# The first chunk's up projection, from seven products of halves to full blocks

## The chip, the cores and the metric

The kernel runs on one core of one Trainium2 chip. The metric is the device time of one execution in microseconds (us), lower is better. The kernel before was timed three times: 1994.26 us median, 1993.06 to 1998.03. A separate profiled execution gives the traces that are read here. Five engines take part: PE (TensorE, the matrix multiplier, whose weight loads are listed apart as PEld), DVE (VectorE), ACT (ScalarE), POOL (GpSimd, idle here) and SP, whose queue issues every DMA of this kernel.

## The reference

One layer of a hybrid decoder over 16 meta tokens and 2048 tokens of width 1024, in float32:

```
h = concat(meta, x)
u = rmsnorm(h, mix_norm_g);  p = u @ w_in                    # W: 1024 -> 1792
y = concat(pool_mixer(p), conformer_conv(p), rglru_branch(p))  # the mixers
h = h + y @ w_out                                            # O
u = rmsnorm(h, mlp_norm_g)                                   # norm2
h = h + square(relu(u @ w_up)) @ w_down                      # U: 1024 -> 4096, D: 4096 -> 1024
out = rmsnorm(h, final_norm_g)[:, 16:]
```

## The kernel before

Everything is held transposed, channels on the 128 partitions and tokens along the free axis. The tokens go in four chunks of 512 (the first also carries the 16 meta tokens). Each chunk passes through W (14 blocks of 128 output channels), the mixers, O (8 blocks), norm2, then four groups g0 to g3, each of U (8 blocks) and D (8 blocks that add onto `h`). The order of these items is written out in the list `items`: W of chunks 0 and 1, O 0, the last three W blocks of chunk 1, then U and D of chunk 0, O 1, W 2, U and D of chunk 1, O 2, and so on. U1 below is U of chunk 1, O1 is O of chunk 1.

Precision is kept by splitting each float32 operand into a rounded high part and a rest (`split`: ACT copies to `hi`, DVE subtracts to get `lo`). A block product is then three matmuls for each of 8 steps of depth: 24 matmuls of 128x512 (`mm_tile`, L278; the first two blocks of a D group go through `mm_pair`, L292, which leaves the last two depth steps to the end). Weights arrive by SP as 128x512 tiles `wr` (6 buffers) and are split into `wh` (4 buffers) by ACT (L110) and DVE (L111). A block needs two such tiles.

U is done otherwise. `up_unit` computes two blocks of 128 channels at once by Strassen's scheme in Winograd's form: seven products of quarter size instead of eight, 12 matmuls of 128x256 each (`mm_block`, L302). It needs sums of the up weights, which `gen_sums` builds on DVE during chunk 0 (L196, L197, L201, L202), stores to DRAM as `sums` and which SP then loads again as weights: of a unit's seven weight tiles four are `sums`. It also needs 14 operand tiles, made by `gen_norm2` (L731 normalises, L738 forms sums, L111 splits), and after the products DVE additions in PSUM order (L795, L820) before ReLU, two squares and one subtraction (L801 to L804) give the two tiles `U` that D reads. Each unit holds four PSUM tiles in use one after the other, and its later products wait for the additions of DVE.

The mixers and the sums are written as generators that hand out pieces of DVE and ACT work. After each item `pump(budget)` draws pieces until their nominal ns use the budget up: 5000 for a W or O item, 3000 for a D item, 150 for a U unit. The list `urgent` comes first (norm2, the sums, the split of the mixers' outputs `gen_ysplit`, the final norm, the next chunk's inputs `gen_x`), the mixers `Mix` after it. At the last U of a chunk `need_mix` issues whatever is left of the next chunk's mixers. Sums for units 0 to 3 are put on the list at O 0, for the next four after each group of U of chunk 0. A scheduler then moves instructions on each engine, so the order below is read from the built program.

At O, `evac_o` adds each block to a tile `xr` of the residual (two buffers, shared with `gen_x`, which loads the chunk after next); `gen_final` stores the finished chunk through the same SP queue.

Of the kernel before, what the change touches and what calls it, by code (L numbers as in the profile page):

```python
# [31 lines left out]
D = 1024  # L32
KB = D // P
# [46 lines left out]
def build(nc, tc, x0, xr, w_in, w_out, w_fold, w_up, w_down, vecs, gates, pools, pws, out):  # L80
# [109 lines left out]
    def gen_sums(u):  # L190

        a11, a12, a21, a22 = (t_(t, W0, n)[:, :512] for t, n in (("s", SBF), ("t", TB), ("t", TB), ("s", SBF)))
        for t, m, c0 in ((a21, 1, 0), (a22, 1, 512), (a11, 0, 0), (a12, 0, 512)):
            nc.sync.dma_start(out=t, in_=w_up[2 * u + m][:, c0 : c0 + 512])
        yield 0
        V.tensor_tensor(out=a22, in0=a21, in1=a22, op=ALU.add)  # L196
        V.tensor_tensor(out=a21, in0=a11, in1=a21, op=ALU.subtract)  # L197
        nc.sync.dma_start(out=sums[u][:, 1536:2048], in_=a22)
        nc.sync.dma_start(out=sums[u][:, 1024:1536], in_=a21)
        yield 1400  # L200
        V.tensor_tensor(out=a11, in0=a22, in1=a11, op=ALU.subtract)  # L201
        V.tensor_tensor(out=a12, in0=a12, in1=a11, op=ALU.subtract)  # L202
        nc.sync.dma_start(out=sums[u][:, 0:512], in_=a11)
        nc.sync.dma_start(out=sums[u][:, 512:1024], in_=a12)
        yield 1400
# [512 lines left out]
    def gen_norm2(o):  # L718
# [54 lines left out]
        for p in range(2):  # L773
            put("B22", p, b22[p])
            put("T4", p, b21[p])
            yield 1400

    def up_unit(o, u, h0):

        fa, fb = a_tile(), a_tile()  # L780
        o.f += [fa, fb]
        ra, rb, t2 = (t_("fr", W0, FR)[:, :NT] for _ in range(3))
        p1 = t_("q", 256, 2)
        order = ("B11", "B21", "T2", "T1", "T3", "B22", "T4")
        nxt = [h0]

        def product(ps):
            h = nxt[0]
            nxt[0] += 1
            wts.ahead(h)  # L790
            mm_block(ps, wts.hl.pop(h), o.u2[order[h - h0]])

        def add2(out, ps, x):

            V.tensor_tensor(  # L795
                out=out.rearrange("p (a c) -> p a c", a=2), in0=ps.rearrange("p (a c) -> p a c", a=2),
                in1=x.unsqueeze(1).broadcast_to([P, 2, 256]), op=ALU.add,
            )

        def square(f, r):  # L800
            A.activation(out=r, in_=r, func=AF.Relu)  # L801
            A.activation(out=f[:, 0], in_=r, func=AF.Square)  # L802
            A.activation(out=r, in_=r, func=AF.Square)  # L803
            V.tensor_tensor(out=f[:, 1], in0=r, in1=f[:, 0].bitcast(F32), op=ALU.subtract)  # L804

        px, py, pz = ps_main(), ps_main(), pw.tile([P, 1024], F32, name=nm("pw"), tag="pw")
        product(px[:, :256])
        A.activation(out=p1, in_=px[:, :256], func=AF.Copy)
        product(py[:, :256])
        product(py[:, 256:])  # L810

        add2(ra, py, p1)
        q = ra[:, 256:]
        product(pz[:, 512:768])
        product(pz[:, 768:])

        add2(t2, pz[:, 512:], q)
        px = ps_main()
        product(px[:, :256])
        V.tensor_tensor(out=q, in0=px[:, :256], in1=t2[:, :256], op=ALU.add)  # L820
        square(fa, ra)
        product(pz[:, 256:512])
        add2(rb, pz[:, 256:768], t2[:, 256:])
        square(fb, rb)

    def evac_d(o, g, j, ps, s0, s1):
# [39 lines left out]
    def pump(budget):  # L866
        credit[0] = min(credit[0], 0) + budget
        while credit[0] > 0:
            v = step()
            if v is None:  # L870
                break
            credit[0] -= v
# [24 lines left out]
    items.extend(("W", 1, b, full) for b in (3, 0, 1))  # L897
    for c in range(NCH):
        for g in range(FG):
            items.extend(("U", c, g * 4 + j, full) for j in range(4))  # L900
            down = [("D", c, g * KB + j, full) for j in range(KB)]
            if g < FG - 1 or c < 2:
                items.extend(down)
            elif c == 2:
                items.extend(down[:2])
                items.extend(("O", 3, j, full) for j in range(KB))
                items.extend(down[2:])
            else:
                for half in ((0, 256), (256, 512)):
                    items.extend(("D", c, g * KB + j, half) for j in range(KB))  # L910
        if c < 2:
            items.extend(("O", c + 1, j, full) for j in range(KB))
            items.extend(("W", c + 2, b, full) for b in range(14))

    def sources(it):

        kind, c, j, _ = it
        if kind == "U":
            m1, m2, s = w_up[2 * j], w_up[2 * j + 1], sums[j]
            aps = (  # L920
                (m1, 0), (m1, 512), (s, 0), (s, 1536), (s, 1024), (s, 512), (m2, 512),
            )
            return ("U", j), [lambda a=a, c0=c0: a[:, c0 : c0 + 512] for a, c0 in aps]
        if kind == "W":
            a = w_in[_WORDER[j][2]]
        elif kind == "D":
            a = w_down[j // KB, j % KB]
        else:
            return ("O", j), [lambda: wo_fold[j], lambda: w_out[j]]
        return (kind, a.offset if hasattr(a, "offset") else j, j), [lambda a=a, c0=c0: a[:, c0 : c0 + 512] for c0 in (0, 512)]  # L930

    srcs, windex, last = [], [], None
    for it in items:
        key, aps = sources(it)
        if it[0] == "W":
            key = ("W", _WORDER[it[2]][2])
        if key != last:
            first = len(srcs)
            srcs.extend(aps)
            last = key  # L940
        windex.append(first)
# [1 line left out]

    gx = {c: (gen_x if c else gen_x0)(ch[c]) for c in range(NCH)}
    gy = {c: gen_ysplit(ch[c]) for c in range(NCH)}
    gn = {c: gen_norm2(ch[c]) for c in range(NCH)}

    next(gx[0])
    mixes.append(Mix(ch[0]))
# [1 line left out]
    for n, it in enumerate(items):  # L951
        kind, c, j, (s0, s1) = it
        o = ch[c]
        if kind == "W":
            need(gx[c])
        elif kind == "O" and j == 0:
            if c == 0:
                urgent.append(gy[0])
            need(gy[c])
            need_mix()  # L960
        elif kind == "U":
            need(gn[c])
        wi = windex[n]
        if kind == "D" and j % KB == 1 and held_ps:
            evac_d(o, j // KB, j % KB, held_ps.pop(), s0, s1)
            pump(BUD_D)
            continue
        if kind == "D" and j % KB == 0 and s0 == 0:
            wts.ahead(wi)
            ws = [[wts.hl.pop(wi + 2 * i + q) for q in range(2)] for i in range(2)]  # L970
            pss = mm_pair(ws, o.f, (s0, s1))
            evac_d(o, j // KB, 0, pss[0], s0, s1)
            held_ps.append(pss[1])
            pump(BUD_D)
            continue
        if kind != "U":
            wts.ahead(wi)
            w = [wts.hl[wi], wts.hl[wi + 1]]
            if n + 1 == len(items) or windex[n + 1] != wi:
                del wts.hl[wi], wts.hl[wi + 1]  # L980
        if kind == "W":
            wk, i, _ = _WORDER[j]
            if n == 0:
                pss = mm_tile(w, o.x, subs_of(o, wk != "z"))
                for _ in gx[0]:
                    pass
                evac_w(o, wk, i, pss)
                urgent.append(gx[1])
                urgent.append(load_consts())
                urgent.append(gen_fold())  # L990
                continue
            evac_w(o, wk, i, mm_tile(w, o.x, subs_of(o, wk != "z")))
        elif kind == "O":
            evac_o(o, j, mm_tile(w, o.u, [full])[0])
            if j == 0 and c == 0:
                urgent.extend(gen_sums(u) for u in range(4))
            if j == KB - 1:
                urgent.append(gn[c])
        elif kind == "U":
            if j % 4 == 0:  # L1000
                o.f = []
            up_unit(o, j, wi)
            if j == 0 and c + 1 < NCH:
                mixes.append(Mix(ch[c + 1]))
            if c == 0 and j % 4 == 3 and j < NU - 1:
                urgent.extend(gen_sums(u) for u in range(j + 1, j + 5))
            if j == NU - 1 and c + 1 < NCH:
                need_mix()
                urgent.append(gy[c + 1])
        else:  # L1010
            ps = mm_tile(w, o.f, [(s0, s1)])[0]
            evac_d(o, j // KB, j % KB, ps, s0, s1)
            if j == FG * KB - 1:
                urgent.append(gen_final(o, s0, s1))
                if c + 2 < NCH:
                    urgent.append(gx[c + 2])
        pump({"U": BUD_U, "D": BUD_D}.get(kind, BUD0))
    while step() is not None:
        pass
    es.close()  # L1020
# [71 lines left out]
```

## Time and profile before

| | us |
|---|---|
| median of 3 runs | 1994.26 |
| profiled execution, its own time | 1989.49 |
| its span, first to last instruction | 1987.7 |
| PE busy in the span | 1927.7 |
| DVE busy | 1580.9 |
| ACT busy | 1127.3 |
| DMA moved | 297.77 MB |

Views of the trace give start and duration in us, the engine, the line of the kernel, the operation, the tile written and the tiles read, shapes and the count of merged instructions. A bracket at the end tells how long the engine stood idle before and what released it. Matmuls overlap, so a group's busy time over its count is longer than the spacing of two matmuls; spacing is read from the starts of following groups. A few per cent of the matmul records can be missing.

### The profile page before, as it was taken

The page shows a single profiled execution, that of the slowest core. Times are in us where ns is not written, and L with a number is a line of the kernel's source. Part 1 is how long each engine was busy: PE and PEld are TensorE (multiplying, and loading weights), DVE is VectorE, ACT ScalarE, POOL GpSimd, SP SyncE. Part 2 cuts the span into 40 slices and gives each one's busy share as a digit, 9 for nine tenths or more (in the row PEclk, how much of TensorE's full clock was granted, in tenths as well). Part 3 has the DMA queues.
Part 4 walks back from the last instruction along what each step waited for, and adds up shares of the span by engine and source line. Part 5 has one row for each costly group of instructions (what it writes and reads, how often), then busy time and mean ns, then how long its engine had stood idle before and what let it go on. Part 6 is the DMA issues. An engine that isn't in the chain of part 4 may idle for free.

```text
span 1987.7 us, 31314 instructions
## 1 busy us (share of the span) xinstructions
PE 1927.7 (97%) x11220; PEld 1685.3 (85%) x11220; DVE 1580.9 (80%) x2557; ACT 1127.3 (57%) x1907; POOL 0.2 (0%) x4
## 2 busy tenths in 40 slices
PE   8999999999999899999999999999999999999997
PEld 7888787888887689898988878988989889889897
DVE  7988787998979899984777689987668587656477
ACT  6575463636586445683666453675648446355364
POOL 0000000000000000000000000000000000000000
PEclk9999999999999999999999999999999999999999
DMA  6415578748443534353534543534445435545354
GB/s 196 133 53 189 181 254 267 254 124 270 125 130 90 186 100 147 110 161 94 165 113 142 172 135 93 163 106 149 132 127 151 135 102 158 162 143 149 112 175 144
DMA packets 166956, 297.77 MB, mean 150 GB/s; under 512 B 18320, under 2 KB 24592, under 8 KB 166800
## 3 DMA queue, kind: packets, MB, share of 16 engines
q1 hardware_dynamic: 166800, 295.77, 48.6%
q8 instruction: 88, 1.44, 0.3%
q14 instruction: 68, 0.56, 0.1%
HBM read 268.43 MB, written 27.26 MB: 149 GB/s over the span
## 4 chain that ended last, share of the span: by engine, by line
PE 73%; DVE 13%; DMA 5%; issue 4%; ACT 4%; SPq 0%; DVEq 0%; ACTq 0%
PE pm L278 41%; PE pm L302 13%; PE pw L302 11%; PE pm L292 7%; DVE wh L111 3%; DMA xr<-d_xr 2%; DMA s<-d_w_up 1%; DVE ca L534 1%; DVE fr L795 1%; ACT wh L110 1%; DVE t L568 1%; PE pb L311 1%; DVE H L111 0%; DVE h L828 0%; DVE U L804 0%
## 5 line engine op out<-in xcount | busy, mean ns | idle before, releaser
L110 ACT ACTIVATE wh<-wr 128x512 fp32r<-128x512 f32 x876 | 546.0, 627 | 669.7 <-PE pm L278 411.5
L278 PE MATMUL pm<-U,wh 128*128 128x512 f32 (+1 forms) x3504 | 790.2, 384 | 1.4 <-DVE wh L111 1.3
L278 PEld LDWEIGHTS pm<-U,wh 128*128 128x128 f32 x3504 | 634.7, 188 | 143.3 <-DVE wh L111 3.1
L111 DVE TENSOR_TENSOR wh<-wr,wh 128x512 fp32r<-128x512 f32 x876 | 598.5, 687 | 187.2 <-ACT wh L110 181.2
L302 PE MATMUL pm<-H,wh 128*128 128x256 f32 x3072 | 392.7, 283 | 4.7 <-DVE wh L111 2.9
L302 PEld LDWEIGHTS pm<-H,wh 128*128 128x128 f32 x3072 | 378.4, 189 | 9.2 <-DVE wh L111 4.4
L302 PE MATMUL pw<-H,wh 128*128 128x256 f32 x2304 | 301.4, 284 | 16.5 <-DVE fr L795 9.2
L302 PEld LDWEIGHTS pw<-H,wh 128*128 128x128 f32 x2304 | 284.9, 190 | 22.3 <-issue 7.2
L278 PE MATMUL pm<-H,wh 128*128 128x512 f32 (+1 forms) x1344 | 272.9, 361 | 13.5 <-ACT H L390 7.3
L278 PEld LDWEIGHTS pm<-H,wh 128*128 128x128 f32 x1344 | 227.7, 193 | 55.7 <-ACT H L390 7.3
L292 PE MATMUL pm<-U,wh 128*128 128x512 f32 (+1 forms) x768 | 176.5, 388 | 0.0
L292 PEld LDWEIGHTS pm<-U,wh 128*128 128x128 f32 x768 | 140.0, 188 | 30.9
L534 DVE SCALAR_TENSOR_TENSOR ca<-Pbv,vec,ca 128x512 f32<-128x512 f32 x180 | 127.0, 745 | 0.0
L828 DVE TENSOR_TENSOR h<-h,pm 128x512 f32<-128x512 f32 (+1 forms) x106 | 71.2, 674 | 49.7 <-PE pm L278 35.9
L804 DVE TENSOR_TENSOR U<-fr,U 128x512 fp32r<-128x512 f32 x128 | 87.3, 685 | 7.9 <-ACT fr L803 7.8
L801 ACT ACTIVATE fr<-fr 128x512 f32<-128x512 f32 x128 | 79.2, 621 | 25.2 <-DVE fr L820 22.5
L795 DVE TENSOR_TENSOR fr<-pw,fr 128x512 f32<-128x512 f32 x128 | 87.8, 686 | 5.5 <-PE pw L302 3.1
L802 ACT ACTIVATE U<-fr 128x512 fp32r<-128x512 f32 x128 | 79.3, 623 | 1.5
L803 ACT ACTIVATE fr<-fr 128x512 f32<-128x512 f32 x128 | 78.7, 618 | 0.3
L346 DVE TENSOR_TENSOR ss<-ss,fr 128x512 f32<-128x512 f32 (+1 forms) x84 | 54.0, 643 | 19.3 <-ACT fr L345 18.2
L337 DVE RECIPROCAL rs<-rs 128x512 f32<-128x512 f32 (+2 forms) x17 | 53.9, 3168 | 10.6 <-ACT rs L335 10.5
L795 DVE TENSOR_TENSOR fr<-pm,q 128x512 f32<-128x512 f32 x64 | 43.7, 683 | 2.8 <-PE pm L302 2.4
(202 smaller groups left out, 1136.3 us busy)
## 6 DMA issues: line engine op xcount, KB each, us to landing
wr<-d_w_down SPq DMA_DIRECT2D x272, 256.0 KB, 3.0
wr<-sums SPq DMA_DIRECT2D x256, 256.0 KB, 3.3
wr<-d_w_up SPq DMA_DIRECT2D x192, 256.0 KB, 3.0
wr<-d_w_in SPq DMA_DIRECT2D x92, 256.0 KB, 2.9
xr<-d_xr SPq DMA_DIRECT2D x56, 256.0 KB, 3.0
t<-d_w_up SPq DMA_DIRECT2D x32, 256.0 KB, 4.0
wr<-wo_fold SPq DMA_DIRECT2D x32, 256.0 KB, 2.7
wr<-d_w_out SPq DMA_DIRECT2D x32, 256.0 KB, 2.7
```

Source lines behind the costliest of these rows:

```text
L110: A.activation(out=hi, in_=src, func=AF.Copy)
L111: V.tensor_tensor(out=lo, in0=src, in1=hi.bitcast(F32), op=ALU.subtract)
L278: T.matmul(ps[:, : s1 - s0], w[k // 4][:, a, (k % 4) * P : (k % 4 + 1) * P], rhs[k][:, b, s0:s1], start=(k == 0 and j == 0), stop=(k == KB ...
L292: T.matmul(ps[:, : s1 - s0], w[k // 4][:, a, (k % 4) * P : (k % 4 + 1) * P], rhs[k][:, b, s0:s1], start=(k == 0 and j == 0), stop=(k == KB ...
L302: T.matmul(ps, w[:, a, k * P : (k + 1) * P], op[k // 2][:, b, (k % 2) * 256 : (k % 2) * 256 + 256], start=(k == 0 and j == 0), stop=(k == ...
L534: V.scalar_tensor_tensor(out=a, in0=o.ub[i][:, k : k + NT], scalar=vc("cw", i * CONVK + k), in1=a, op0=ALU.mult, op1=ALU.add)
L795: V.tensor_tensor(out=out.rearrange("p (a c) -> p a c", a=2), in0=ps.rearrange("p (a c) -> p a c", a=2), in1=x.unsqueeze(1).broadcast_to([ ...
L801: A.activation(out=r, in_=r, func=AF.Relu)
L802: A.activation(out=f[:, 0], in_=r, func=AF.Square)
L803: A.activation(out=r, in_=r, func=AF.Square)
L804: V.tensor_tensor(out=f[:, 1], in0=r, in1=f[:, 0].bitcast(F32), op=ALU.subtract)
L828: V.tensor_tensor(out=h, in0=h, in1=ps[:, : s1 - s0], op=ALU.add)
```

## The change

U of chunk 0 no longer uses the seven products. A new `gen_norm2_0` makes eight plain normalised and split tiles (L785), each block is one `mm_tile` of 24 matmuls of 128x512, and `up_block` takes ReLU straight from PSUM on ACT, then squares as before (the subtraction is now L794). The items of U in chunk 0 become 32 blocks instead of 16 units and get the budget of D (3000). The sums are still all made, four units after each group of U of chunk 0, in place of four at O 0 and four after each of the first three groups. Chunks 1 to 3 compute as before.

```diff
+    def gen_norm2_0(o):
+        rs = rsqrt_of([colsum(o.ss2[:, :NT])], [(0, NT)], 1.0 / D)
+        yield 3300
+        o.u2 = []
+        for k in range(KB):
+            raw = t_("s", W0, SBF)[:, :NT] if k % 2 else t_("t", W0, TB)[:, :NT]
+            V.scalar_tensor_tensor(out=raw, in0=o.h[k][:, :NT], scalar=vc("g2", k), in1=rs[:, :NT], op0=ALU.mult, op1=ALU.mult)
+            t = b_tile()
+            split(t[:, 0, :NT], t[:, 1, :NT], raw)
+            o.u2.append(t)
+            yield 1400
+
+    def square(f, r):
+        A.activation(out=f[:, 0], in_=r, func=AF.Square)
+        A.activation(out=r, in_=r, func=AF.Square)
+        V.tensor_tensor(out=f[:, 1], in0=r, in1=f[:, 0].bitcast(F32), op=ALU.subtract)
+
+    def up_block(o, ps):
+        f, r = a_tile(), t_("fr", W0, FR)[:, :NT]
+        o.f.append(f)
+        A.activation(out=r, in_=ps, func=AF.Relu)
+        square(f, r)
...
         for g in range(FG):
-            items.extend(("U", c, g * 4 + j, full) for j in range(4))
+            n = 4 if c else 8
+            items.extend(("U", c, g * n + j, full) for j in range(n))
...
-        if kind == "U":
+        if kind == "U" and c:
             m1, m2, s = w_up[2 * j], w_up[2 * j + 1], sums[j]
...
+        elif kind == "U":
+            a = w_up[j]
...
             evac_o(o, j, mm_tile(w, o.u, [full])[0])
-            if j == 0 and c == 0:
-                urgent.extend(gen_sums(u) for u in range(4))
...
-            up_unit(o, j, wi)
+            if c:
+                up_unit(o, j, wi)
+            else:
+                up_block(o, mm_tile(w, o.u2, [full])[0])
             if j == 0 and c + 1 < NCH:
                 mixes.append(Mix(ch[c + 1]))
-            if c == 0 and j % 4 == 3 and j < NU - 1:
-                urgent.extend(gen_sums(u) for u in range(j + 1, j + 5))
-            if j == NU - 1 and c + 1 < NCH:
+            if c == 0 and j % n == n - 1:
+                urgent.extend(gen_sums(u) for u in range(j // n * 4, j // n * 4 + 4))
+            if j == FG * n - 1 and c + 1 < NCH:
                 need_mix()
                 urgent.append(gy[c + 1])
...
-        pump({"U": BUD_U, "D": BUD_D}.get(kind, BUD0))
+        pump({"U": BUD_U if c else BUD_D, "D": BUD_D}.get(kind, BUD0))
```

The order of instructions moves at three places that matter below. First, DVE behind the reciprocal of chunk 0's norm2 (`rs`), with `h` the residual, `H` the operand tiles of U and `wh` split weights. Before:

```order
L337 RECIPROCAL rs_2235<-rs_2235 128x512
...
L738 TENSOR_TENSOR t_2252<-s_2354,t_2252 128x512
L738 TENSOR_TENSOR t_2299<-t_2299,t_2252 128x512
L111 TENSOR_TENSOR H_2240<-t_2252,H_2240 128x512
L111 TENSOR_TENSOR H_2245<-t_2257,H_2245 128x512
L738 TENSOR_TENSOR t_2257<-s_2358,t_2257 128x512
L738 TENSOR_TENSOR t_2304<-t_2304,t_2257 128x512
L111 TENSOR_TENSOR H_2241<-t_2257,H_2241 128x512
L111 TENSOR_TENSOR wh_2490<-wr_2368,wh_2490 128x512
```

and now:

```order
L337 RECIPROCAL rs_2171<-rs_2171 128x512
...
L111 TENSOR_TENSOR H_2233<-t_2231,H_2233 128x512
L111 TENSOR_TENSOR H_2275<-s_2273,H_2275 128x512
L785 SCALAR_TENSOR_TENSOR t_2278<-h_2118,vec_69,rs_2171 128x512
L111 TENSOR_TENSOR wh_2390<-wr_2242,wh_2390 128x512
L785 SCALAR_TENSOR_TENSOR s_2283<-h_2160,vec_69,rs_2171 128x512
L111 TENSOR_TENSOR H_2280<-t_2278,H_2280 128x512
L111 TENSOR_TENSOR H_2285<-s_2283,H_2285 128x512
L111 TENSOR_TENSOR wh_2393<-wr_2244,wh_2393 128x512
```

The tile `H_2241` stood 39 instructions behind the reciprocal, with six more operand splits still to come; the last of the eight tiles now, `H_2285`, stands 22 behind it.

Second, DVE where a group of sums is made. Before, in U of group g2:

```order
L196 TENSOR_TENSOR s_5025<-t_5024,s_5025 128x512
L111 TENSOR_TENSOR wh_4568<-wr_4446,wh_4568 128x512
L804 TENSOR_TENSOR U_4377<-fr_4379,U_4377 128x512
L111 TENSOR_TENSOR wh_4586<-wr_4463,wh_4586 128x512
L795 TENSOR_TENSOR fr_4526<-pm_4531,q_4529 128x512
L111 TENSOR_TENSOR wh_4603<-wr_4482,wh_4603 128x512
L197 TENSOR_TENSOR t_5024<-s_5022,t_5024 128x512
L795 TENSOR_TENSOR fr_4528<-pw_4532,fr_4526 128x512
```

and now, across the border from U to D of group g0 (L849 adds a D block onto `h`):

```order
L196 TENSOR_TENSOR s_2749<-t_2748,s_2749 128x512
L111 TENSOR_TENSOR wh_2856<-wr_2659,wh_2856 128x512
L794 TENSOR_TENSOR U_2740<-fr_2741,U_2740 128x512
L197 TENSOR_TENSOR t_2748<-s_2746,t_2748 128x512
...
L849 TENSOR_TENSOR h_1868<-h_1868,pm_2772 128x512
L111 TENSOR_TENSOR wh_2862<-wr_2711,wh_2862 128x512
L197 TENSOR_TENSOR t_2825<-s_2823,t_2825 128x512
L111 TENSOR_TENSOR wh_2865<-wr_2713,wh_2865 128x512
```

The additions that feed the next product of a unit (L795) no longer stand behind the sums; what stands behind them is split weights, the last tile of a group and additions onto `h`.

Third, DVE at the end of D of group g3, ahead of O1 (L598, L618: the last of the mixers; `H` here: their outputs, split for O1; L714: the first block of O1). Before:

```order
L598 SCALAR_TENSOR_TENSOR Pcx_1168<-t_6038,st_15_103,t_6008 128x512
L111 TENSOR_TENSOR H_6158<-ca_4273,H_6158 128x512
...
L618 SCALAR_TENSOR_TENSOR Pz_1767<-Pz_1767,Pcx_1168 128x512
...
L111 TENSOR_TENSOR H_6180<-Pz_1767,H_6180 128x512
L346 TENSOR_TENSOR ss_6153<-ss_6153,fr_6268 128x512
...
L828 TENSOR_TENSOR h_2224<-h_2224,pm_6398 128x512
...
L714 TENSOR_TENSOR h_6474<-pm_6446,xr_6472 128x512
```

and now, from inside U of group g3 on:

```order
L111 TENSOR_TENSOR H_5313<-Pz_1767,H_5313 128x512
L794 TENSOR_TENSOR U_4987<-fr_4988,U_4987 128x512
...
L849 TENSOR_TENSOR h_1868<-h_1868,pm_5072 128x512
...
L849 TENSOR_TENSOR h_2118<-h_2118,pm_5365 128x512
...
L849 TENSOR_TENSOR h_2160<-h_2160,pm_5404 128x512
L346 TENSOR_TENSOR ss_5123<-ss_5123,fr_5430 128x512
...
L714 TENSOR_TENSOR h_5480<-pm_5452,xr_5478 128x512
```

The mixers of chunk 1 and the split of their outputs now stand ahead of the last tiles of U; D of g3 has only its own additions and the squares of the final norm.

More of the change, by code (lines that the diff above doesn't have):

```diff
@@ L798, in add2 @@
             )
[L800 to L804, printed above, removed]
         px, py, pz = ps_main(), ps_main(), pw.tile([P, 1024], F32, name=nm("pw"), tag="pw")
@@ L820, in up_unit @@
         V.tensor_tensor(out=q, in0=px[:, :256], in1=t2[:, :256], op=ALU.add)
+        A.activation(out=ra, in_=ra, func=AF.Relu)
         square(fa, ra)
@@ L823, in up_unit @@
         add2(rb, pz[:, 256:768], t2[:, 256:])
+        A.activation(out=rb, in_=rb, func=AF.Relu)
         square(fb, rb)
@@ L934, in build @@
         key, aps = sources(it)
+        if it[0] == "U":
+            key = ("U", it[1] > 0, it[2])
         if it[0] == "W":
@@ L945, in build @@
     gy = {c: gen_ysplit(ch[c]) for c in range(NCH)}
-    gn = {c: gen_norm2(ch[c]) for c in range(NCH)}
+    gn = {c: (gen_norm2 if c else gen_norm2_0)(ch[c]) for c in range(NCH)}
     next(gx[0])
@@ L975, in build @@
             continue
-        if kind != "U":
+        if kind != "U" or c == 0:
             wts.ahead(wi)
@@ L999, in build @@
         elif kind == "U":
-            if j % 4 == 0:
+            n = 4 if c else 8
+            if j % n == 0:
                 o.f = []
-            up_unit(o, j, wi)
+            if c:
+                up_unit(o, j, wi)
+            else:
+                up_block(o, mm_tile(w, o.u2, [full])[0])
             if j == 0 and c + 1 < NCH:
                 mixes.append(Mix(ch[c + 1]))
-            if c == 0 and j % 4 == 3 and j < NU - 1:
-                urgent.extend(gen_sums(u) for u in range(j + 1, j + 5))
-            if j == NU - 1 and c + 1 < NCH:
+            if c == 0 and j % n == n - 1:
+                urgent.extend(gen_sums(u) for u in range(j // n * 4, j // n * 4 + 4))
+            if j == FG * n - 1 and c + 1 < NCH:
                 need_mix()
```

## The prediction

> **What bounds the kernel now.** I read the page first, then the chain of waits, then the timeline of PE through chunk 0.
>
> ```profile
> PE 1927.7 (97%) x11220; PEld 1685.3 (85%) x11220; DVE 1580.9 (80%) x2557; ACT 1127.3 (57%) x1907; POOL 0.2 (0%) x4
> PE 73%; DVE 13%; DMA 5%; issue 4%; ACT 4%; SPq 0%; DVEq 0%; ACTq 0%
> ```
>
> PE sets the end nearly everywhere, so a change counts by the PE work it adds and the PE gaps it closes. The spacing of matmuls comes from the undisturbed U and D of chunk 3:
>
> ```profile
> 1720.03 4.44 PE L302 MATMUL pm<-H,wh 128*128 128x256 f32 x36
> 1730.00 4.43 PE L302 MATMUL pm<-H,wh 128*128 128x256 f32 x36
> ...
> 1844.58 11.36 PE L292 MATMUL pm<-U,wh 128*128 128x512 f32 x48
> 1855.78 4.59 PE L278 MATMUL pm<-U,wh 128*128 128x512 f32 x19
> ```
>
> From one unit to the next are 9.97 us for 84 matmuls of 256 columns, 0.1187 us each; 48 matmuls of 512 columns take 11.20 us, 0.2333 each. A dense group of U is 4 x 9.97 = 39.9 us, a dense group of D 8 x 24 x 0.2333 = 44.8. Chunk 0 is not dense. Here are the starts of its stages, and two of its gaps:
>
> ```profile
> 243.12 3.00 PE L302 MATMUL pm<-H,wh 128*128 128x256 f32 x24
> 246.26 0.39 PE L302 MATMUL pw<-H,wh 128*128 128x256 f32 x1
> 251.00 1.15 PE L302 MATMUL pw<-H,wh 128*128 128x256 f32 x5 [4.35 <-DVE H L111]
> ...
> 294.02 11.31 PE L292 MATMUL pm<-U,wh 128*128 128x512 f32 x48
> ...
> 341.49 0.40 PE L302 MATMUL pm<-H,wh 128*128 128x256 f32 x2
> ...
> 389.99 11.33 PE L292 MATMUL pm<-U,wh 128*128 128x512 f32 x48
> ...
> 434.61 0.39 PE L311 MATMUL pb<-hl,c_gw 128*128 128x512 f32 x1
> ...
> 436.01 4.45 PE L302 MATMUL pm<-H,wh 128*128 128x256 f32 x36
> ...
> 457.97 1.65 PE L302 MATMUL pw<-H,wh 128*128 128x256 f32 x12 [3.16 <-DVE fr L795]
> ...
> 479.62 11.31 PE L292 MATMUL pm<-U,wh 128*128 128x512 f32 x48
> ...
> 524.23 4.67 PE L302 MATMUL pm<-H,wh 128*128 128x256 f32 x36
> ...
> 569.60 10.15 PE L292 MATMUL pm<-U,wh 128*128 128x512 f32 x43
> ...
> 620.36 1.89 PE L278 MATMUL pm<-H,wh 128*128 128x512 f32 x6
> ```
>
> U and D of the four groups take 50.9 and 47.5, 48.5 and 46.0, 43.6 and 44.6, 45.4 and 50.8 us: together 377.2 from 243.12 to 620.36. Dense they would be 4 x (39.9 + 44.8) = 338.7, and chunk 1's mixers put 30 small matmuls in between (24 of the gates, 6 of column sums), six of which take 1.40 us (434.61 to 436.01), so 7.0. The rest, 377.2 - 338.7 - 7.0 = 31.5 us, is PE held up, 27 of it in U. The timeline of DVE shows by whom:
>
> ```profile
> 231.46 3.35 DVE L337 RECIPROCAL rs<-rs 128x512 f32<-128x512 f32 x1 [1.31 <-ACT rs L335]
> ...
> 456.53 0.69 DVE L197 TENSOR_TENSOR t<-s,t 128x512 f32<-128x512 f32 x1 [1.98 <-DMA s<-d_w_up]
> ```
>
> At 456.53 the addition a unit needs (L795) sat behind a sum that waited for its load; PE resumed at 457.97. In the first group the 14 operand tiles were late.
>
> The second loose place is O1, set beside O2, the same stage one chunk later:
>
> ```profile
> 626.59 11.32 PE L278 MATMUL pm<-H,wh 128*128 128x512 f32 x41 [2.93 <-DVE H L111]
> ...
> 673.40 0.79 PE L327 MATMUL pb<-hl,ones 128*128 128x512 f32 x1 [6.03 <-ACT hl L110]
> ...
> 681.90 6.67 PE L278 MATMUL pm<-U,wh 128*128 128x512 f32 x28
> ...
> 1110.20 3.17 PE L278 MATMUL pm<-H,wh 128*128 128x512 f32 x13
> ...
> 1151.69 0.50 PE L327 MATMUL pb<-hl,ones 128*128 128x512 f32 x1 [1.86 <-ACT hl L110]
> ...
> 1160.09 7.27 PE L278 MATMUL pm<-U,wh 128*128 128x512 f32 x30
> ```
>
> O1 took 61.5 us (620.36 to 681.90), O2 49.9, for the same 192 matmuls.
>
> ```profile
> 626.45 2.49 DVE L111 TENSOR_TENSOR H<-Pz,H 128x512 fp32r<-128x512 f32 x4
> ...
> 632.08 0.68 DVE L828 TENSOR_TENSOR h<-h,pm 128x512 f32<-128x512 f32 x1
> ```
>
> DVE was still splitting the mixers' outputs for O1 six us after O1 began, and added D's last block at 632.08, nearly 12 us after PE had left D. From there a chain runs on: final norm, stores, the next chunk's inputs through the two `xr` buffers, and the column sum on which PE stood 6.03 us at 673.40.
>
> **The change, part by part.**
>
> *PE work.* Removed: 16 units x 84 x 0.1187 = 159.5 us. Added: 32 blocks x 24 x 0.2333 = 179.2. That is 19.6 us more, on the path. By this alone the profiled 1989.5 would become 2009. The mixers' 7.0 us only change places.
>
> The Trainium skill ("TensorE: Matmul & The Clock Gate", Back-to-back issue gap) gives an isolated gap of N/2.4 + 2.5 ns, 215.8 and 109.2 ns, by which the added work is an estimate of 19.0 us; the same section has 131 ns as sustained spacing at N=512, by which full blocks would be far cheaper; the rows above, 233 ns, speak against that figure.
>
> *U's own gaps.* The 27 us go where their causes go. The first group: the reciprocal ends at 234.81 and W covers PE until 243.12. By the order of DVE the last of eight tiles stands 22 instructions behind it, 8 normalisations and 14 splits. A split takes 2.49 / 4 = 0.62; a 512-wide operation with a scalar at most
>
> ```profile
> L534 DVE SCALAR_TENSOR_TENSOR ca<-Pbv,vec,ca 128x512 f32<-128x512 f32 x60 | 42.3, 744 | 0.0
> ```
>
> 0.74. So 14 x 0.62 + 8 x 0.74 = 14.6, ready at 249.4; PE wants it seven eighths into its first block, 243.12 + 21 x 0.2333 = 248.0, later if the scheduler draws matmuls of the second block ahead, as the order shows. I take 1 us, between 0 and 2.5.
>
> In the other groups nothing on PE waits inside a block, and a finished block leaves through ACT; only the last tile of a group is wanted soon, and D's first two blocks leave its depth step to the end (36 matmuls, 8.4 us). What can still hold PE is split weights behind a waiting sum:
>
> ```profile
> DVE t L197 <- DMA s<-d_w_up: 12.1, 5, 3.6
> ```
>
> That is the longest wait of DVE from 243 to 570, five times, at most 3.6 us. Two blocks' weights lie split ahead, 11.2 us of PE. I take 1 us for the three groups together.
>
> *DVE's load.* A block of U now costs three splits, 1.9 us, plus 3 us of mixers per 5.6 us. A group of D costs 16 weight splits, 8 additions, 16 sum operations (40 x 0.62 = 24.8) and some 13 of mixers: 38 of 44.8. Both fit. The mixers are drawn earlier: their nominal pieces add up to some 106 us, the 12 units of sums before the last D to 12 x 2.8 = 34; budgets up to the end of U g3 are 32 x 3 + 24 x 3 = 168, before 16 x 0.15 + 72 = 74. Before, some 65 us were left to the last U; now nothing is, and the order shows the last split of a mixer output inside U g3.
>
> *D's gaps.* Of 31.5 us D has 4.5: 47.5 - 44.8 - 0.5 in g0 and 50.8 - 44.8 - 3.7 (16 small matmuls) in g3, none in g1 and g2. All four will have sums nearby. SP passes each unit's loads and stores in order with the weights, so late stores delay weights; ten tiles are asked for ahead, 28 us of PE, and chunk 0's U asks for 64 tiles in place of 112. I take 3 us, between 0 and 2.2 a group, 8.8.
>
> So U and D last 179.2 + 179.2 + 7.0 + 5 = 370.4 in place of 377.2: 6.8 us less, between 11.8 less and, with 2.5 + 3 x 1 + 8.8 = 14.3 of gaps, 2.5 more.
>
> *O1.* With the mixers done, DVE adds D's last block as it comes, and O1 has O2's conditions: the same loads, stores and order of the column sum. I take 49.9, 11.6 us less. The bound below is no gain.
>
> The clock is part of these gaps:
>
> ```profile
> 243.00:294.00 51.00, 44.63 (x338) 42.66 (x337) 48.71 (x84) 33.23 (x62) 0.00 (x0) 0.93 0.71 231
> 620.40:681.90 61.50, 50.68 (x197) 38.80 (x196) 50.40 (x72) 31.40 (x54) 0.00 (x0) 0.92 0.50 157
> 1110.20:1160.10 49.90, 47.81 (x198) 37.42 (x196) 39.83 (x54) 24.67 (x41) 0.00 (x0) 0.97 0.59 190
> ```
>
> The column before the last two is the granted clock: 0.93 in U g0 and 0.92 in O1, where 7% of 51 and 8% of 61.5 make 3.6 and 4.9 us of lost clock; in O2 1.5. These lie inside the stage lengths used, and are not added again.
>
> *The sum.* 6.8 + 11.6 = 18.4 us less: profiled 1989.5 to 1971.1. The median of the runs shown is 4.8 above the profiled execution; carrying that over, 1994.3 - 18.4 = 1976.
>
> **The rivals.**
>
> *A: O1 stays slow.* Stores and loads share SP there:
>
> ```profile
> 646.55 4.25 SPq L840 DMA_DIRECT2D d_out<-h  x6
> ...
> 652.34 0.34 SPq L411 DMA_DIRECT2D xr<-d_xr  x1
> ```
>
> An input load follows six stores, and two `xr` buffers serve 16 loads. If that queue and not the late DVE sets O1, only 6.8 us are won: 1987. Against it: O2 has the same queue and took 49.9.
>
> *B: slower.* The idle time stays while PE's work grows. The sums are as many, their loads, stores and the weights share one SP queue and DVE is in order; if split weights come late behind them in every group, U and D keep 31.5 us of gaps, the mixers' outputs for O1 come behind the sums of units 12 to 15, and the added 19.6 stands alone: 1994.3 + 19.6 = 2014. It decides from the point where gaps in U and D pass 11.8 + 11.6 = 23.4 us with O1 repaired, or 11.8 without. For it: DVE sat 12.1 us on those loads. Against it: D of g1 and g2 ran dense at 46.0 - 1.4 and 44.6 us with sums under way in g2.
>
> *C: the change does less than it says*: U runs dense, but the mixers, not the sums, keep DVE late, so that D and O1 lose half of what they gain: 6.8 + 5.8 = 12.6 less, 1982. It lies inside the range.
>
> **How the numbers follow.** Forecast 0.65, C 0.12, A 0.15, B with its milder forms 0.08. A difference under 0.3% (6 us) cannot be told from none here. Forecast and C are faster; of A I count 0.09 faster and 0.06 the same, of B 0.02 the same and 0.06 slower: 0.86, 0.08, 0.06. The range goes from all gaps gone, 23.4 us less (1971), and a median 4 us nearer to the profiled time, to 1967, and up to A with two us more gap, 1989. Outside are B and the tails, under 2 in 10.
>
> **What would show it.** Right: U groups of chunk 0 at 44.8 to 46 us with spacing 0.2333; first U block starting near 243 with a gap under 2.5; no wait of PE for L795-like additions before chunk 1; mixers' splits before D of g3 ends; the final norm's column sum a few us after O1 begins and O1 near 50 us; the granted clock from 200 to 700 near 1.00; from W2 on the traces alike but shifted. Wrong: PE waiting in D for `wh` behind L197 or the stores of sums (B), or O1 still above 58 us with DVE idle (A).

## The result, and the profile after

The changed kernel takes 1970.2 us (median of 4 runs, 1967.3 to 1971.46) against 1993.93 (4 runs): a ratio of 0.9878, 95% interval 0.9865 to 0.9891. The profiled execution went from 1989.49 to 1969.41, its span from 1987.7 to 1967.6. It was forecast at 1976, range 1967 to 1989, and faster.

The page of the changed kernel, its first part and its chain:

```profile
PE 1932.1 (98%) x10644; PEld 1664.2 (85%) x10644; DVE 1510.1 (77%) x2423; ACT 1099.2 (56%) x1839; POOL 0.2 (0%) x4
PE 82%; DVE 9%; DMA 4%; ACT 2%; issue 2%; SPq 0%; DVEq 0%; ACTq 0%
```

PE is busy 4.4 us longer in a span 20.1 us shorter, and its share of the chain of waits rose from 73% to 82%. DVE lost 71 us. The timeline of PE shows the stages (start, duration, count, idle time before):

```profile
243.26 21.75 PE L278 MATMUL pm<-H,wh 128*128 128x512 f32 x93
266.54 0.50 PE L327 MATMUL pb<-hl,ones 128*128 128x512 f32 x1 [1.54 <-ACT hl L110]
...
290.04 11.32 PE L292 MATMUL pm<-U,wh 128*128 128x512 f32 x48
...
336.12 16.81 PE L278 MATMUL pm<-H,wh 128*128 128x512 f32 x72
...
381.91 11.44 PE L292 MATMUL pm<-U,wh 128*128 128x512 f32 x48
...
398.32 19.32 PE L278 MATMUL pm<-U,wh 128*128 128x512 f32 x82 [1.73 <-DVE wh L111]
...
430.07 11.26 PE L278 MATMUL pm<-H,wh 128*128 128x512 f32 x48
...
476.81 11.32 PE L292 MATMUL pm<-U,wh 128*128 128x512 f32 x48
...
521.42 44.56 PE L278 MATMUL pm<-H,wh 128*128 128x512 f32 x192
565.82 11.32 PE L292 MATMUL pm<-U,wh 128*128 128x512 f32 x48
...
610.43 3.18 PE L278 MATMUL pm<-H,wh 128*128 128x512 f32 x13
...
652.01 0.50 PE L327 MATMUL pb<-hl,ones 128*128 128x512 f32 x1 [1.81 <-ACT hl L110]
653.16 0.50 PE L328 MATMUL pb<-hl,ones 128*128 128x512 f32 x1 [0.65 <-DVE hl L111]
654.47 7.33 PE L278 MATMUL pm<-H,wh 128*128 128x512 f32 x24 [0.80 <-DVE h L714]
661.63 7.14 PE L278 MATMUL pm<-U,wh 128*128 128x512 f32 x30
```

U and D of chunk 0 last 610.43 - 243.26 = 367.2 us in place of 377.2, O1 51.2 in place of 61.5; W2 begins 20.3 us earlier, and from there the traces run alike to an end 20.1 us earlier. So the gain lies wholly between 243 and 682, half in U and D and half in O1. Two gaps of PE are left in U and D, 1.54 and 1.73 us.

### The profile page after: what moved, and what is told of

Its sections match the earlier page's. It is cut to its first block, busy times and chain, and to the rows that moved or that the text cites. A ratio compares the mean times of both kernels' runs of the same rounds, so it can differ in the third digit from the quotient of the medians.

```text
span 1967.6 us, 29715 instructions
## 1 busy us (share of the span) xinstructions
PE 1932.1 (98%) x10644; PEld 1664.2 (85%) x10644; DVE 1510.1 (77%) x2423; ACT 1099.2 (56%) x1839; POOL 0.2 (0%) x4
## 3 DMA queue, kind: packets, MB, share of 16 engines
q1 hardware_dynamic: 159888, 283.18, 46.3%
## 4 chain that ended last, share of the span: by engine, by line
PE 82%; DVE 9%; DMA 4%; ACT 2%; issue 2%; SPq 0%; DVEq 0%; ACTq 0%
PE pm L278 52%; PE pm L302 11%; PE pw L302 9%; PE pm L292 8%; DVE wh L111 2%; DMA xr<-d_xr 2%; DVE ca L534 1%; DMA s<-d_w_up 1%; DVE fr L820 1%; DVE t L568 1%; PE pb L311 0%; ACT wh L110 0%; DMA wr<-d_w_down 0%; DVE U L149 0%; PE pb L312 0%
## 5 line engine op out<-in xcount | busy, mean ns | idle before, releaser
L110 ACT ACTIVATE wh<-wr 128x512 fp32r<-128x512 f32 x828 | 517.3, 627 | 713.8 <-PE pm L278 490.5
L111 DVE TENSOR_TENSOR wh<-wr,wh 128x512 fp32r<-128x512 f32 x828 | 566.5, 688 | 209.0 <-ACT wh L110 204.4
L278 PE MATMUL pm<-H,wh 128*128 128x512 f32 (+1 forms) x2112 | 449.9, 372 | 9.6 <-ACT H L390 7.3
L278 PEld LDWEIGHTS pm<-H,wh 128*128 128x128 f32 x2112 | 370.8, 190 | 84.1 <-ACT H L390 7.3
L302 PE MATMUL pm<-H,wh 128*128 128x256 f32 x2304 | 292.3, 282 | 2.3 <-DVE wh L111 1.4
L302 PEld LDWEIGHTS pm<-H,wh 128*128 128x128 f32 x2304 | 282.2, 188 | 5.2 <-DVE wh L111 2.2
L302 PE MATMUL pw<-H,wh 128*128 128x256 f32 x1728 | 223.2, 283 | 1.6 <-DVE fr L820 1.6
L302 PEld LDWEIGHTS pw<-H,wh 128*128 128x128 f32 x1728 | 212.0, 189 | 4.7 <-DVE fr L820 4.0
L849 DVE TENSOR_TENSOR h<-h,pm 128x512 f32<-128x512 f32 (+1 forms) x106 | 71.5, 674 | 60.5 <-PE pm L278 45.6
L794 DVE TENSOR_TENSOR U<-fr,U 128x512 fp32r<-128x512 f32 x128 | 87.5, 685 | 11.4 <-ACT fr L793 11.4
L793 ACT ACTIVATE fr<-fr 128x512 f32<-128x512 f32 x128 | 79.3, 621 | 1.1
L820 DVE TENSOR_TENSOR fr<-pw,fr 128x512 f32<-128x512 f32 x96 | 66.0, 687 | 4.5 <-PE pw L302 1.9
L534 DVE SCALAR_TENSOR_TENSOR ca<-h,vec,ca 128x512 f32<-128x512 f32 x60 | 42.7, 746 | 0.0
L840 ACT ACTIVATE fr<-fr 128x512 f32<-128x512 f32 x48 | 30.0, 624 | 12.2 <-DVE fr L839 11.8
```

The costliest lines, as they stand in the source:

```text
L110: A.activation(out=hi, in_=src, func=AF.Copy)
L111: V.tensor_tensor(out=lo, in0=src, in1=hi.bitcast(F32), op=ALU.subtract)
L278: T.matmul(ps[:, : s1 - s0], w[k // 4][:, a, (k % 4) * P : (k % 4 + 1) * P], rhs[k][:, b, s0:s1], start=(k == 0 and j == 0), stop=(k == KB ...
L302: T.matmul(ps, w[:, a, k * P : (k + 1) * P], op[k // 2][:, b, (k % 2) * 256 : (k % 2) * 256 + 256], start=(k == 0 and j == 0), stop=(k == ...
L534: V.scalar_tensor_tensor(out=a, in0=o.ub[i][:, k : k + NT], scalar=vc("cw", i * CONVK + k), in1=a, op0=ALU.mult, op1=ALU.add)
L820: V.tensor_tensor(out=out.rearrange("p (a c) -> p a c", a=2), in0=ps.rearrange("p (a c) -> p a c", a=2), in1=x.unsqueeze(1).broadcast_to([ ...
```

## The experiments

The stages in each profiled execution, in us, from the starts of stages as above, and the medians. Ratios are to the kernel before on the same chip. A profiled execution need not lie at its median: that of "blocks, low budget" took 1992.78 us and is the slowest of its ten, that of "units, budget" took 1984.2 and is the slowest of its four, that of "units, budget from g1" took 1974.16 and is the fastest of its four.

| kernel | U, D of chunk 0 | O1 | O2 | median | ratio (95%) |
|---|---|---|---|---|---|
| before | 377.2 | 61.5 | 49.9 | 1993.93 | |
| changed | 367.2 | 51.2 | 49.8 | 1970.2 | 0.9878 (0.9865 to 0.9891) |
| units, no sums | 359.8 | 48.7 | | 1961.76 | 0.9843 (0.9818 to 0.9867) |
| blocks, no sums | 365.1 | 49.9 | | 1964.79 | 0.9857 (0.9837 to 0.9878) |
| blocks, low budget | 370.4 | 71.2 | | 1986.89 | 0.9969 (0.9954 to 0.9983) |
| blocks, sums early | 365.8 | 52.3 | | 1969.82 | 0.9879 (0.9857 to 0.9902) |
| changed, again | 367.0 | 49.5 | 48.2 | 1966.54 | 0.9867 (0.9852 to 0.9882) |
| units, budget | 381.4 | 50.0 | 49.7 | 1981.17 | 0.9941 (0.9926 to 0.9956) |
| units, budget from g1 | 376.1 | 48.8 | 48.5 | 1980.41 | 0.9930 (0.9906 to 0.9954) |
| two chunks in blocks | 367.4 | 48.9 | 47.6 | 1981.08 | 0.9941 (0.9924 to 0.9957) |
| before, three `xr` | 377.8 | 53.5 | 46.5 | 1977.39 | 0.9918 (0.9902 to 0.9935) |
| units, budget, three `xr` | 374.4 | 46.3 | 46.1 | 1966.05 | 0.9859 (0.9842 to 0.9876) |
| blocks, three `xr` | 365.6 | 47.4 | 46.6 | 1960.58 | 0.9837 (0.9822 to 0.9852) |

The main theory: in units, the sums and the 14 operands hold PE through DVE, and the late mixers hold O1; the blocks take PE out of reach of the first and let the mixers be drawn earlier.

**The price of the sums, in units and in blocks.** Both kernels without `gen_sums`; the edit of the units is shown, and the changed kernel loses its own call of `gen_sums` in the same way:

```diff
-                (m1, 0), (m1, 512), (s, 0), (s, 1536), (s, 1024), (s, 512), (m2, 512),
+                (m1, 0), (m1, 512), (m2, 0), (m1, 512), (m2, 0), (m1, 0), (m2, 512),
...
-                urgent.extend(gen_sums(u) for u in range(4))
...
-                urgent.extend(gen_sums(u) for u in range(j + 1, j + 5))
```

> The kernel before with no sums made or stored: the units of all chunks load parts of the up weights in place of the sums, as many tiles, so the output of the up projection is not the reference's. Theory (sums hold VectorE and with it the units' own additions): the gaps of U in groups g1 to g3 of chunk 0, 16.5 us, and of D, 4.5 us, go; the first group keeps about 10 us because its 14 operand tiles are late all the same; the mixers get the budget of the sums and O1 falls by some 8 us. Together 25 to 30 us less than before, near 1966. Rival (the units wait for their own chain of additions, sums or not): U of chunk 0 stays near 188 us and at most 8 us are won.

> The changed kernel with no sums made or stored; chunks 1 to 3 load parts of the up weights in their place, so their output is not the reference's. Theory (with full blocks the sums lie beside other work): 0 to 3 us less than the changed kernel, the gap in D of group g1 (1.73 us) goes. Rival (the sums still cost in D and O1): 6 us or more less.

Units without sums: 32 us of median under the kernel before, a little more than the 25 to 30 expected. Between the profiled executions the span is 27.9 us shorter; U and D are shorter by 17.4 (377.2 to 359.8) and O1 by 12.8, where some 8 had been expected, and the other stages give 2.3 back. The first group of U and the waits of PE from 243 to 604 in this kernel:

```profile
243.98 3.00 PE L302 MATMUL pm<-H,wh 128*128 128x256 f32 x24
...
293.92 11.33 PE L292 MATMUL pm<-U,wh 128*128 128x512 f32 x48
```

```profile
PE pw L302 <- DVE H L111: 4.6, 2, 4.4
PE pw L302 <- DVE fr L795: 1.9, 2, 1.5
```

What stays is the first group, 49.9 us against a dense 39.9: its operands are late with or without sums. The unit's own additions cost PE 1.9 us in this stretch. So the sums, not the form of the unit, held U from g1 on. The run takes away their work on DVE, their loads and their stores together, so which of these held U most is not separated. O1 gained because the mixers got the budget of the sums: the last of their outputs was split by 593.3, ahead of the end of D at 603.8, where the kernel before was still splitting at 628.

```profile
591.99 1.29 DVE L111 TENSOR_TENSOR H<-Pz,H 128x512 fp32r<-128x512 f32 x2
```

Blocks without sums win 3.2 us of span on the profiled execution of the changed kernel, 1964.4 against 1967.6, 2.1 of it in U and D; by the ratios the median is some 4 us lower. That is at the edge of the theory's 0 to 3: sums that cost units about 30 us cost blocks 2 to 5. And without sums units would beat blocks by 3 to 5 us: the blocks pay because the sums must be made just then.

**The budget alone.** The changed kernel with the old budget for U:

```diff
-        pump({"U": BUD_U if c else BUD_D, "D": BUD_D}.get(kind, BUD0))
+        pump({"U": BUD_U, "D": BUD_D}.get(kind, BUD0))
```

> The changed kernel, but U of chunk 0 draws mixers with the old budget of 150 for each item, now 32 x 150. Theory (O1 was slow because the mixers came late): U and D of chunk 0 up to D of g3 as in the changed kernel, D of g3 longer by 2 us or more, O1 near 60 us in place of 51.2, so 9 to 14 us slower than the changed kernel, 1980 to 1984. Rival (O1 gains from the lighter load of VectorE and the shorter SP queue, whatever the budget): within 3 us of the changed kernel.

It lost 16.7 us of median to the changed kernel's first runs, more than the 9 to 14 expected. U and D stay within 3.2 us, O1 grows to 71.2; as the slowest of ten executions was profiled, 5.9 us over the median, O1 is probably shorter in most of them. PE in O1 of this kernel:

```profile
614.23 2.11 PE L278 MATMUL pm<-H,wh 128*128 128x512 f32 x8
622.23 6.29 PE L278 MATMUL pm<-H,wh 128*128 128x512 f32 x15 [5.89 <-DVE H L111]
...
662.87 8.49 PE L278 MATMUL pm<-H,wh 128*128 128x512 f32 x24 [3.67 <-DVE h L714]
675.42 0.67 PE L327 MATMUL pb<-hl,ones 128*128 128x512 f32 x1 [4.06 <-ACT hl L110]
```

and DVE at the same time:

```profile
619.08 0.69 DVE L111 TENSOR_TENSOR H<-ca,H 128x512 fp32r<-128x512 f32 x1
...
629.72 0.69 DVE L111 TENSOR_TENSOR H<-Pz,H 128x512 fp32r<-128x512 f32 x1
...
632.12 0.69 DVE L849 TENSOR_TENSOR h<-h,pm 128x512 f32<-128x512 f32 x1
```

The mixers' outputs are split while O1 should run, and the last addition of D falls 18 us after D. In the changed kernel the splits end at 563 and the last addition at 611:

```profile
563.18 0.69 DVE L111 TENSOR_TENSOR H<-Pz,H 128x512 fp32r<-128x512 f32 x1 [0.35 <-ACT H L110]
...
610.63 0.69 DVE L849 TENSOR_TENSOR h<-h,pm 128x512 f32<-128x512 f32 x1 [1.38 <-PE pm L278]
```

Late mixers make O1 slow; that step is shown.

**Where the sums are made.** Blocks with the sums in their old places:

```diff
+            if j == 0 and c == 0:
+                urgent.extend(gen_sums(u) for u in range(4))
...
-            if c == 0 and j % n == n - 1:
-                urgent.extend(gen_sums(u) for u in range(j // n * 4, j // n * 4 + 4))
+            if c == 0 and j % n == n - 1 and j < FG * n - 1:
+                urgent.extend(gen_sums(u) for u in range(j // n * 4 + 4, j // n * 4 + 8))
```

> The changed kernel with the sums made where they were before: four units at O 0, four after each of the first three groups of U of chunk 0. Theory (with full blocks PE does not wait for what stands behind the sums, wherever they are): within 3 us of the changed kernel. Rival (moving the sums out of O 0 and norm2 is what freed the first group): the first U of chunk 0 starts with a gap of 3 us or more and the time is 5 us or more longer.

0.9879 against 0.9878: no difference. The part of the change that moves the sums behind each group of U does nothing by itself.

**The same on one chip, and the early mixers with units.** The changed kernel was run once more beside the next three:

> The changed kernel once more, beside the next ones on the same chip: 0.988 of the kernel before, 1968 to 1972.

0.9867. The median, 1966.54, lies 1.5 us below the range expected, and the two intervals of the ratio overlap; between two sets of runs of this kernel a few us are not a difference. Then the kernel before, with one edit:

```diff
-        pump({"U": BUD_U, "D": BUD_D}.get(kind, BUD0))
+        pump({"U": BUD_U if c else 3000, "D": BUD_D}.get(kind, BUD0))
```

> The kernel before, with one edit: a unit of U of chunk 0 draws 3000 ns of mixers in place of 150. Theory (VectorE has no room in units: a unit costs it 8.7 of its 9.97 us, so that drawing the mixers earlier only moves the delay): U of chunk 0 grows by 15 us or more over its 188, O1 falls from 61.5 to about 50, in all no gain, 1990 to 2010. Rival (the early mixers alone bring the 10 us of O1, units or blocks): 1980 to 1986.

The rival is right. U and D grew by 4.2 us, not 15, O1 fell to 50.0, and 12.3 us of median are won with units as they were. The changed kernel wins 26.9 on the same chip, so about half of its gain is to be had by the budget alone. That DVE has no room in units was wrong. A part of the 4.2 us is one wait in the first group:

```profile
300.02 0.79 PE L327 MATMUL pb<-hl,ones 128*128 128x512 f32 x1 [6.06 <-ACT hl L110]
```

The early mixers bring a column sum into the order of PE, the one for the norm of chunk 1's inputs, and PE waits there for its input. ACT, which squares these inputs, had itself waited for their loads into `xr`:

```profile
294.34 1.27 ACT L345 ACTIVATE fr<-xr 128x512 f32<-128x512 f32 x2 [3.09 <-DMA xr<-d_xr]
```

To avoid it, the budget was held back in the first group:

```diff
-        pump({"U": BUD_U if c else 3000, "D": BUD_D}.get(kind, BUD0))
+        pump({"U": BUD_U if c or j < 4 else 3000, "D": BUD_D}.get(kind, BUD0))
```

> The units with 3000 ns of mixers each from the second group on, 150 in the first. Theory (in the first group VectorE is busy with the 14 operand tiles, and mixers drawn there delay it): the first group falls from 59 back to about 51 us, the later ones stay near 42 to 44, O1 near 50, in all 4 to 8 us less than with the budget in all groups, 1973 to 1977. Rival (the mixers' work only moves to the later groups): within 2 us of 1981.

The stages of its profiled execution are as the theory has them (first group 50.7, U and D 376.1, O1 48.8), and that execution took 1974.16, but the median is 1980.41 with runs up to 1984.79: by its number the rival was right, and the run is not told apart from the budget in all groups.

**The price of blocks where nothing is to be repaired.** U of chunk 1 in blocks too (every test on the chunk in the change reads `c < 2` in place of `c == 0`):

```diff
-            n = 4 if c else 8
+            n = 4 if c > 1 else 8
...
-            if c:
+            if c > 1:
                 up_unit(o, j, wi)
```

> The changed kernel with U of chunk 1 in full blocks too. Theory (blocks add 19.6 us of PE work a chunk, and chunk 1 has hardly a gap to give back): 15 to 20 us slower than the changed kernel, 1985 to 1991. Rival (blocks are better in themselves, because their additions do not stand between products): the same as the changed kernel or faster.

14.5 us slower than the changed kernel beside it, half a us short of the band. U and D of chunk 1 last 1090.23 - 740.57 = 349.7 in the changed kernel and 1102.91 - 740.32 = 362.6 here, by the first rows of U1 and O2 of each:

```profile
740.57 4.45 PE L302 MATMUL pm<-H,wh 128*128 128x256 f32 x36
...
1090.23 3.18 PE L278 MATMUL pm<-H,wh 128*128 128x512 f32 x13
```

```profile
740.32 16.81 PE L278 MATMUL pm<-H,wh 128*128 128x512 f32 x72
...
1102.91 3.19 PE L278 MATMUL pm<-H,wh 128*128 128x512 f32 x13
```

Blocks are not better in themselves; they cost 12.9 us net in chunk 1, which by the 18 us of PE work added (see below) gave back some 5 us of small gaps.

**The rest of O1 and O2.** A third `xr` buffer in the changed kernel:

```diff
-    def w_raw(src, tag="xr", bufs=2):
+    def w_raw(src, tag="xr", bufs=3):
...
-            raw = t_("xr", NT, 2)
+            raw = t_("xr", NT, 3)
```

> The changed kernel with three buffers for xr in place of two. Theory (what is left of the gaps in O1 and O2, some 5 us each, is the chain of 16 loads through two buffers): O1 and O2 near 47, 4 to 8 us faster than the changed kernel. Rival (the loads stand behind the stores of the finished chunk in the queue of SP): O1 and O2 within 1 us of 51 and 50, the time within 2 us.

0.9837 against 0.9867 on the same chip, 6.0 us: O1 is 2.1 us shorter and O2 1.6. U begins 1.9 us earlier (241.95 against 243.83), but that is not shown to be the buffer's: among kernels with two buffers this start lies between 242.41 and 245.40, and the kernel before begins U at 243.15 with the third buffer and at 243.12 without. Run again it gave 0.9838 (1961.37 us):

> The changed kernel with three xr buffers once more: 0.984 of the kernel before, 1959 to 1963.

This version is the fastest measured that does all of the work. To see whose gain the buffer takes, it was given to the kernel before and to the units with the early mixers:

> The kernel before with three xr buffers and nothing else. Theory (O1 of the kernel before was slow because the mixers came late, and the buffers only add to it): U and D of chunk 0 lose up to 7 us as they did with the units and the budget, O2 3 us, O1 stays above 55 us; 1978 to 1986. Rival (the two buffers were what made O1 slow): O1 near 47, 1968 to 1974.

> The units with 3000 ns of mixers each and three xr buffers. Theory (units keep the price of the sums and of the 14 operands, some 14 us against blocks; the third buffer helps O1, O2 and the start alike): about 6 us less than the units with the budget alone, 1973 to 1977, and 12 to 16 us behind the blocks with three buffers (1960.6). Rival (what the blocks gained lay in O1 and its buffers only): within 5 us of the blocks with three buffers.

Alone it brought 16 us of median and 12.1 of span, 11.4 of these in O1 and O2: O1 53.5, O2 46.5, U and D unchanged at 377.8. Both statements missed: O1 is below the theory's 55 and above the rival's 47, and U and D gained nothing. So O1 of the kernel before had two causes that overlap, late mixers and two buffers; of 61.5 - 46.3 = 15.2 us that both repair together, the buffer alone repairs 8.0 and the budget alone 11.5. With both, units come to 1966.05, 4.7 us behind the blocks run beside them, so by its number the rival was right here; but the stages tell them apart: U and D take 374.4 in units and 365.7 in blocks, O1 46.3 and 47.5. The 8.7 us in U and D are what the blocks still bring then, and O1 takes 1.2 of them back. With two buffers the blocks are worth 14.6 us of median over units with the early mixers. The third buffer made the difference small because U and D of the units fell from 381.4 to 374.4. Of these 7.0 us 5.9 lie in U and D of the first group (244.64 to 354.94 against 242.82 to 347.19), where the wait for the column sum fell from 6.06 to 3.26:

```profile
293.70 0.78 PE L327 MATMUL pb<-hl,ones 128*128 128x512 f32 x1 [3.26 <-ACT hl L110]
```

Its input comes through `xr`, so this part fits the buffer. DVE's waits for loads of the sums fell too; what the rest is due to, no run isolates.

## Why the prediction was right

*PE work, 19.6 us.* Right in kind and 8% too large. A dense group of blocks ran from 521.42 to 565.82, 44.40 us or 0.2313 a matmul, where 0.2333 was taken from D; by 0.2313 the blocks add 177.6 - 159.5 = 18.1 us. The two-chunk run fits: 12.9 us, and chunk 1 had some gaps to give.

*The first group, a gap of 0 to 2.5, taken as 1.* The last operand tile was split by 249.8 where 249.4 had been worked out, and PE did not wait for it:

```profile
231.65 3.35 DVE L337 RECIPROCAL rs<-rs 128x512 f32<-128x512 f32 x1 [1.31 <-ACT rs L335]
...
249.09 0.69 DVE L111 TENSOR_TENSOR H<-s,H 128x512 fp32r<-128x512 f32 x1
```

What the prediction had not listed is the wait of 1.54 us at 266.54: the column sum of chunk 1's inputs now sits inside this group. It is the same wait that cost units 6.06 us. So the size of this term came out near by luck: the cause that it priced cost nothing, and another one took its place.

*The gaps of U and D, 5 us.* By the prediction's own count of PE work 367.2 - 365.4 = 1.8. With U's measured spacing that work is 1.6 us smaller, and 3.4 us of gaps are left, in the main the two waits of 1.54 and 1.73. D was to keep 3 us, from weights that come late behind stores, and kept one gap, 1.73 us at 398.32. It was made in the way that the prediction had described for U and priced at 1 us there: DVE waited for a load of the sums and a weight split stood behind it.

```profile
396.31 0.69 DVE L196 TENSOR_TENSOR s<-t,s 128x512 f32<-128x512 f32 x1 [2.03 <-DMA s<-d_w_up]
...
397.59 0.68 DVE L111 TENSOR_TENSOR wh<-wr,wh 128x512 fp32r<-128x512 f32 x1
```

DVE's waits for the sums did not shrink; from 243 to 612 they were

```profile
DVE t L197 <- DMA s<-d_w_up: 15.6, 6, 4.7
...
DVE s L196 <- DMA s<-d_w_up: 6.0, 3, 2.4
```

against 12.1 in the kernel before for the first and, for the second, from 243 to 570:

```profile
DVE s L196 <- DMA s<-d_w_up: 1.7, 1, 1.7
```

Only who stands behind them has changed, as the prediction argued. So U and D gained 10.1 us where 6.8 were forecast. Of the 3.3 us between them, half is the spacing of the matmuls in U and half the gaps, both sized too large.

*O1, 11.6 us.* 10.3 came. That the mixers' lateness was the cause is shown by the low budget, which undoes just this. The claim that O1 would then have O2's conditions held (51.2 and 49.8; 49.5 and 48.2 in the second run). Rival A, that the queue of stores and loads sets O1, was wrong as the main cause but not empty: the third buffer shows that the loads cost both stages about 2 us, and that it could have repaired half of O1 without the change.

*The sum.* 18.4 us forecast and 20.1 measured between the profiled executions, U and D 3.3 better than forecast and O1 1.3 worse. The forecast of 1976 misses the median by 5.8 us: 1.7 from the sum, and 4 from carrying the 4.8 us between median and profiled execution over to the changed kernel, whose median lies 0.8 above its profiled one. The range had been drawn with that. Two of the signs did not come out as stated: U groups took 46.8, 45.8, 46.7 and 44.4 us where 44.8 to 46 was given, since the prediction had not placed the small matmuls and the column sum there, and the granted clock in O1 was 0.97.

*Rivals.* B needed PE to wait behind the sums in every group; it did once. C's half gain of O1 did not appear. What the forecast left out is that the two gains are separable: it put O1's to the change, where a number in the budget table brings it too.

## What to carry to other kernels

Before an algorithm that saves multiplier work by more additions is kept, look at who else uses the adding engine in that stage: here 18 us less of PE work came with 27 us of waiting in the one chunk in which the sums of the weights were being made and the 14 operand tiles came late, and paid in the chunk after it. What a wait of an engine costs depends on what is queued behind it: the sums cost U and D some 17 us with a product's additions behind them on DVE, and about 2 us with work behind them that has two blocks of slack, although DVE waited longer for their loads then. And when a change moves a budget along with an algorithm, run the budget alone: here it was half of the gain.

## What the runs showed of the hardware

In U of the changed kernel a matmul of 128x512 took 0.2313 us (44.40 us for 192, from 521.42), and in the D group before it 0.2323 (44.61 us for 192, from 476.81); the D of chunk 3 from which the prediction took its spacing has 0.2333. We know of no cause. The granted clock in the first group rose from 0.93 to 1.00, and in O1 from 0.92 to 0.97:

```profile
243.00:290.00 47.00, 45.46 (x196) 36.35 (x195) 39.26 (x66) 32.67 (x56) 0.00 (x0) 1.00 0.54 169
...
610.40:661.60 51.20, 47.94 (x197) 37.71 (x196) 40.53 (x54) 26.56 (x43) 0.00 (x0) 0.97 0.57 185
```

The first stretch has one gap of 1.54 us and no loss of clock; O1 has gaps of 1.81, 0.65 and 0.80 us close together. The Trainium skill ("TensorE: Matmul & The Clock Gate", Part 1: The HAM clock gate) has the clock halved after an idle window of about 3.4 us. The first stretch agrees; in O1 no single gap is that long, and the trace shows that less was enough. Here are two stretches of 3.41 us of O1, one behind the other, with the time that PE was busy as the second number and the clock as the last but two:

```profile
650.89:654.30 3.41, 1.01 (x2) 0.37 (x2) 2.80 (x5) 1.66 (x4) 0.00 (x0) 1.00 0.79 235
654.30:657.71 3.41, 3.24 (x8) 2.57 (x9) 3.40 (x3) 0.72 (x2) 0.00 (x0) 0.50 0.48 151
```

The clock stood at half for the second, which cost O1 about 1.7 us, and in the first PE was busy for 1.01 us. In O1 of "units, budget" even 2.02 busy us of 3.41 were followed by half the clock:

```profile
666.29:669.70 3.41, 2.02 (x6) 1.23 (x7) 3.27 (x6) 2.46 (x5) 0.00 (x0) 1.00 0.54 201
669.70:673.12 3.42, 3.42 (x9) 2.63 (x8) 3.00 (x1) 0.13 (x1) 0.00 (x0) 0.50 0.44 149
```

The second run of the changed kernel has gaps of 1.95, 0.65 and 0.46 us at this place and kept the full clock:

```profile
652.55 0.50 PE L327 MATMUL pb<-hl,ones 128*128 128x512 f32 x1 [1.95 <-ACT hl L110]
653.71 0.50 PE L328 MATMUL pb<-hl,ones 128*128 128x512 f32 x1 [0.65 <-DVE hl L111]
654.66 5.83 PE L278 MATMUL pm<-H,wh 128*128 128x512 f32 x24 [0.46 <-DVE h L714]
```

```profile
610.80:660.30 49.50, 46.44 (x197) 36.62 (x196) 39.99 (x54) 25.98 (x43) 0.00 (x0) 1.00 0.59 191
```

So a mostly idle stretch of 3.4 us can be enough, and the length of the gaps alone does not decide; what else does, no run here isolates. A loss of this size is also what lies between the two runs in O1, 51.2 and 49.5.
